# Down projection by seven half-size products in three of its four rounds

## The chip, the core and the metric

The kernel runs on one core of a Trainium2 chip, as one launch. The metric is the device time of that launch in microseconds (us). Five engines of the core matter here: TensorE (PE, matrix products; its weight loads are listed as PEld), VectorE (DVE), ScalarE (ACT), GpSimd (POOL) and the DMA queues, which are fed by SyncE (SP) and by GpSimd. Each engine takes its instructions in the order in which the program issues them, and waits on semaphores where an operand is not ready.

## What is computed

The reference is one decoder layer on 512 tokens of width 1024, in float32. The change touches its two feed-forward blocks only:

```python
D_MODEL = 1024; SEQ = 512; D_FF = 2816
def swiglu(x, w_gate, w_up, w_down):
    return (jax.nn.silu(x @ w_gate) * (x @ w_up)) @ w_down
h = h + 0.5 * swiglu(rms_norm(h, g_ffn1[i]), w_ffn1_gate[i], w_ffn1_up[i], w_ffn1_down[i])
...                                    # gated convolution and three-group attention, then
h = h + 0.5 * swiglu(rms_norm(h, g_ffn2[i]), w_ffn2_gate[i], w_ffn2_up[i], w_ffn2_down[i])
h = h + sigmoid(rmsnorm(h) @ W_pg) * (p[i] @ W_pp)
y = rmsnorm_final(h)
```

## The kernel before, in words

**Numbers.** Every matrix product is done three times at a reduced float32 (type fp32r): a weight w is split in wh (rounded) and wl (the rest), data in the same way, and wh·xh, wh·xl and wl·xh are added up in PSUM (`mm3`, L386). A weight is split by ACT (rounding) and DVE (the rest), or, for the products in `BY_DMA` and the slabs in `RAISED`, by ACT twice and an adding DMA that GpSimd issues: ACT writes -wh into wl, and the DMA adds w to it (`remainder`, L313). Such a slab is ready only when that DMA has landed.

**Layout.** Data lie transposed: a tile of 128 partitions holds 128 features, its 512 columns are the tokens. D_FF has 22 chunks of 128 features, which the code takes as 11 pairs j. Stationary operands are 128x128 blocks of weights; 1024 columns of them are a slab (`W`, 16 buffers, L232). All tiles of data come from one pool of 61 (`T`, L150).

**Gate and up.** The first two pairs (`EARLY`) are computed plainly with 512-column matmuls while the norm is still under way (`plain`, L573). For the other nine, gate and up together are a 2x2 block product: weights in quarters A11 to A22 (the two halves of the 1024 inputs for gate and for up), tokens in two halves. The block product is done by seven half-size products instead of eight (`PRODUCTS`, L66). The data's sums and differences of blocks are formed once (`normed`, L596); those of the weights are formed for each pair by four DVE operations (`sum_one`, L266). Each product is 4 x 2 x 3 = 24 matmuls of 256 columns, into one of three PSUM banks (pa, pe, pd), several products on top of each other; after each product the bank is read by ACT (copy) or DVE (sum), before the next product that adds to it (`gate_up`, L666). The hidden chunks of a pair are then split into hidh and hidl (`keep`, L566).

**Down.** Hidden chunks are multiplied by the down weights in three rounds of 8, 8 and 6 chunks. For each of the 8 output tiles m a round makes 8 x 3 (or 6 x 3) matmuls of 512 columns into a bank pd, and DVE adds half of it to the residual (`down`, L714). In the last round the residual is also split for the next stage and squared for its norm (`into`, L757).

**Order.** `PLAN` (L70) writes out the order of gate/up pairs and down rounds. Slabs are loaded, summed and split a fixed number of slabs ahead of their use (`slab`, L371): splitting by DMA begins 4 slabs ahead (`EARLIER`), the other splits 2 ahead. Small work is queued as `jobs`, and `work` (L554) takes them as far as an account of ACT and DVE time allows. The rotary tables of the attention (32 DVE operations, `tables`, L779) are put between the products of the first block from pair 3 on.

Of the kernel before, what the change touches and what calls it, by code (L numbers as in the profile page):

```python
# [52 lines left out]

N_TAB = {3: 1, 4: 1, 5: 1, 6: 1}
EARLIER = 4
MORE = 1
# [43 lines left out]

def ffn_order(n):
    out = [("gq", n, j, q) for j in range(EARLY) for q in range(4)]
    for step in PLAN:
        if step[0] == "gu":
            out += [(n, step, q) for q in PRODUCTS]
        else:
            out += [("d" + n, m, step[1]) for m in range(*step[2:])]
    return out
# [24 lines left out]
def block_kernel(ctx: ExitStack, tc: tile.TileContext, a, out):  # L133
    nc = tc.nc
    V, A, PE, G = nc.vector, nc.scalar, nc.tensor, nc.gpsimd

# [45 lines left out]
    def quarter(n, j, q):  # L182

        x_, y = divmod(q, 2)
        w = a["w_ffn%s_%s" % (n, ("gate", "up")[x_])]
        return [w[2 * j + i][:, y * S:(y + 1) * S] for i in range(2)]

    def source(key):
        kind = key[0]
        if kind in ("d1", "d2"):  # L190
            ks = ROUNDS[key[2]]
            return a["w_ffn%s_down" % kind[1]][key[1]][:, ks[0] * P:(ks[-1] + 1) * P]
# [8 lines left out]
    def sources(key):  # L201
# [7 lines left out]
        if key[0] == "gq":  # L209
            return row_of(quarter(*key[1:]))  # L210
# [42 lines left out]
    def load_one(hold=False):  # L253
# [5 lines left out]
        elif q == "B11":  # L259
            for z in (A21, A22, A11):  # L260
                quarters[key[:2], z] = fetch(row_of(quarter(key[0], key[1][1], z)))
        elif q == "B21":
            quarters[key[:2], A12] = fetch(row_of(quarter(key[0], key[1][1], A12)))
        state["load"] = i + 1

    def sum_one():  # L266
# [13 lines left out]
        if q in PRODUCTS[:4]:  # L280
            spend(0, 0.17 + w * 0.001)
        if q == "B11":
            r = z(A11)
            mixed[k, 1] = W("s1")[:, :w]
            V.tensor_add(mixed[k, 1], z(A21), z(A22))
        elif q == "B21":
            r = z(A12)
            mixed[k, 2] = W("s2")[:, :w]
            V.tensor_sub(mixed[k, 2], mixed[k, 1], z(A11))
        elif q == "T2":  # L290
            r = mixed[k, 2]
            s3 = z(A21, True)
            V.tensor_sub(s3, z(A11, True), s3)
            mixed[k, 3] = s3
        elif q == "T1":
            r = mixed.pop((k, 1))
            mixed[k, 4] = W("s4")[:, :w]
            V.tensor_sub(mixed[k, 4], z(A12, True), mixed.pop((k, 2)))
        elif q == "T3":
            r = mixed.pop((k, 3))  # L300
        elif q == "B22":
            r = mixed.pop((k, 4))
        else:
            r = z(A22, True)
# [65 lines left out]

    def slab(key):  # L371
# [4 lines left out]
        for j in range(i + 1, i + AHEAD + sums + 1):  # L376
            ahead("load", load_one, j + 1)
            ahead("sum", sum_one, j + 1)
            ahead("early", early_one, min(j, i + EARLIER) + 1)
            ahead("split", split_one, min(j, i + AHEAD) + 1)  # L380
        ahead("load", load_one, i + AHEAD + RAW + 1)
# [51 lines left out]
    def begin(norm):  # L433
# [8 lines left out]
        def piece(j, queue):  # L442
            for i, c in cuts[j]:
                g, at = divmod(c.start, S)
                src = quarter("1", 0, (A11, A12)[i])[g]
# [97 lines left out]
    jobs = []  # L543

    def job(f, a_=0.0, v=0.0):

        jobs.append((f, a_, v))

    def next_job():
        f, a_, v = jobs.pop(0)  # L550
        spend(a_, v)
        f()
# [7 lines left out]
    def ffn(n, xs, norm, resid, after):  # L560
        lo, hi = slice(0, 256), slice(256, 512)
        hid = []
        spare = []
        xn = [None] * 4

        def keep(ts):  # L566
            hl = [(T("hidh", F32R), T("hidl", F32R)) for _ in ts]
            for t, (h, l) in zip(ts, hl):
                job(lambda t=t, h=h: A.activation(h, t, AF.Copy), 0.63)
            for t, (h, l) in zip(ts, hl):  # L570
                job(lambda t=t, h=h, l=l: (V.tensor_sub(l, t, h.bitcast(F32)), hid.append((h, l))), v=0.69)
# [13 lines left out]
        def gated(pgs, pus, R):  # L585
# [8 lines left out]
            keep(tu)  # L594

        def normed(R):  # L596
# [26 lines left out]
            for c in range(4):  # L623
                xn[c] = {}
# [23 lines left out]
        for j in range(EARLY):  # L648
# [9 lines left out]
            gated(*done, R)  # L658
# [6 lines left out]

        def gate_up(j):  # L666
# [4 lines left out]
            us_ = W("u")  # L671
            both = us_.rearrange("p (c s) -> p c s", s=S)

            for q in PRODUCTS:
# [4 lines left out]
                for k in range(4):  # L679
                    th, tl = xn[k][q]  # L680
                    for g in range(2):
                        c = slice((g * 4 + k) * P, (g * 4 + k + 1) * P)
                        mm3(p[:, g * 256:(g + 1) * 256], h[:, c], l[:, c], th, tl,
                            q in ("B11", "B21", "T1") and k == g == 0, k == 3, True)
                m = N_TAB.get(j, 0) if n == "1" else 0
                background(m)
                spend(0, 0.7 * m)
                if j > EARLY:
# [5 lines left out]
                elif q == "T4":  # L694
                    while "gate" not in t:
# [4 lines left out]
                    keep([both[:, i] for i in range(2)])  # L700
                else:
# [5 lines left out]
                    elif q == "B22":  # L707
                        job(lambda z=z: A.activation(z, z, AF.Silu), 0.63)
                        job(lambda: V.tensor_mul(both[:, :, hi], t["T1"].rearrange("p (c s) -> p c s", s=256),
                                                 t["T2"].rearrange("p (c s) -> p c s", s=256)), 0, 0.69)  # L710
                if j == EARLY:
                    work(2.88)

        def down(r, first_, end):  # L714
            ks = ROUNDS[r]
            if n == "1" and r == len(ROUNDS) - 1:
                spare.append(T("h"))
            for m in range(first_, end):
                while len(hid) <= ks[-1] and m > first_:
                    next_job()  # L720
                p = bank("pd")
                key = "d" + n, m, r
                h, l = slab(key)
                for i, k in enumerate(ks):
# [747 lines left out]
```

## Time and profile before

| | |
|---|---|
| median of 3 runs | 1300.3 us (1300.05 to 1300.98) |
| the profiled execution's own time | 1300.78 us |
| its span (first to last instruction) | 1298.7 us |
| PE busy | 1285.4 us, 99% of the span |
| weight loads (PEld) | 1141.1 us, 88% |
| DVE busy | 835.1 us, 64% |
| ACT busy | 689.4 us, 53% |
| POOL busy (all of it DMA issues) | 231.9 us, 18% |
| mean granted TensorE clock | 0.998 |

The row of an instruction gives its start and its duration. [...] A group's row gives the busy time of the group, the mean of one instruction in ns, and the idle time in front of it with what ended it.

### The profile page before, as it was taken

The numbers are of one execution on the slowest core, as the hardware profiler recorded it, in microseconds if no ns is written. First come the engines' busy times: TensorE is split into PE (matmuls) and PEld (weight loads), VectorE is DVE, ScalarE is ACT, GpSimd is POOL, SyncE is SP. The second block draws the span as 40 slices with busy tenths as digits, with TensorE's granted clock in tenths as the row PEclk, the third lists the DMA queues.
The fourth block names the chain that finished last, engine by engine and source line by source line (L and its number), as shares of the span: only waits on it lengthen the run. The fifth ranks groups of instructions, "written<-read, shape, count | busy, mean of one in ns | idle before, by whom it ended". The sixth has DMA issues, their size and how long they took to land.

```text
span 1298.7 us, 19406 instructions
## 1 busy us (share of the span) xinstructions
PE 1285.4 (99%) x7474; PEld 1141.1 (88%) x7474; DVE 835.1 (64%) x1379; ACT 689.4 (53%) x989; POOL 231.9 (18%) x302
## 2 busy tenths in 40 slices
PE   9999999999999999999999999999999999999996
PEld 7899899898888888989898888888998899898886
DVE  6985567362559887878778757555972366352565
ACT  6667276565533264746556345343765367474552
POOL 3111111112232232323322210001102111111000
PEclk9999999999999999999999999999999999999999
DMA  9668766969888889898897782325669676868641
GB/s 300 144 158 228 195 154 160 227 149 223 203 200 199 201 149 197 166 186 152 173 182 169 175 226 86 97 92 137 146 149 251 169 181 156 216 161 199 158 103 60
DMA packets 106404, 223.35 MB, mean 172 GB/s; under 512 B 19272, under 2 KB 41160, under 8 KB 106312
## 3 DMA queue, kind: packets, MB, share of 16 engines
q0 software_dynamic: 47008, 135.29, 51.5%
q1 hardware_dynamic: 59016, 86.56, 21.2%
q8 instruction: 59, 0.97, 0.3%
q14 instruction: 33, 0.27, 0.1%
q10 hardware_dynamic: 288, 0.26, 0.1%
HBM read 164.36 MB, written 2.13 MB: 128 GB/s over the span
## 4 chain that ended last, share of the span: by engine, by line
PE 93%; DMA 3%; issue 2%; DVE 1%; ACT 0%; POOL 0%; SPq 0%; ACTq 0%; POOLq 0%; DVEq 0%
PE pd L387 8%; PE pd L388 8%; PE pd L389 8%; PE pa L389 6%; PE pa L387 6%; PE pa L388 6%; PE pq L387 4%; PE pq L388 4%; PE pq L389 4%; PE pg L387 3%; PE pg L388 3%; PE pg L389 3%; DMA wl<-wr 2%; PE pb L387 2%; PE pb L388 2%
## 5 line engine op out<-in xcount | busy, mean ns | idle before, releaser
L318 POOL DMA_DIRECT2D wl<-wr x106 | 91.3, 864 | 522.6 <-ACT wl L316 473.4
L862 DVE SCALAR_TENSOR_TENSOR acc<-glu,taps,acc 128x511 f32<-128x511 f32 (+14 forms) x240 | 161.5, 731 | 0.0
L316 ACT ACTIVATE wl<-wr 128x1024 fp32r<-128x1024 f32 (+1 forms) x106 | 108.1, 1020 | 80.1 <-DMA wl<-wr 40.6
L387 PE MATMUL pd<-hidh,wh 128*128 128x512 f32 x352 | 137.0, 389 | 0.0
L388 PE MATMUL pd<-hidl,wh 128*128 128x512 f32 x352 | 137.0, 389 | 0.0
L389 PE MATMUL pd<-hidh,wl 128*128 128x512 f32 x352 | 136.9, 389 | 0.0
L389 PE MATMUL pa<-bh,wl 128*128 128x256 f32 x432 | 122.7, 284 | 0.3 <-DVE wl L347 0.3
L387 PE MATMUL pa<-bh,wh 128*128 128x256 f32 x432 | 122.3, 283 | 0.4 <-ACT p L692 0.4
L388 PE MATMUL pa<-bl,wh 128*128 128x256 f32 x432 | 122.2, 283 | 0.0
L330 ACT ACTIVATE wh<-wr 128x1024 fp32r<-128x1024 f32 (+1 forms) x106 | 107.6, 1015 | 27.0 <-DMA wl<-wr 24.1
L347 DVE TENSOR_TENSOR wl<-s,wh 128x1024 fp32r<-128x1024 f32 x54 | 66.0, 1221 | 64.9 <-ACT wh L346 64.8
L316 ACT ACTIVATE wl<-wh 128x1024 fp32r<-128x1024 f32 x76 | 79.7, 1051 | 50.2 <-DMA wh<-in_w_in 38.9
L387 PE MATMUL pq<-xsh,wh 128*128 128x512 f32 x224 | 88.7, 396 | 0.0
L318 POOL DMA_DIRECT2D wl<-in_w_in x56 | 48.2, 860 | 222.1 <-ACT wl L316 221.0
L388 PE MATMUL pq<-xsl,wh 128*128 128x512 f32 x224 | 87.3, 390 | 0.0
L389 PE MATMUL pq<-xsh,wl 128*128 128x512 f32 x224 | 87.3, 390 | 0.0
L389 PEld LDWEIGHTS pa<-bh,wl 128*128 128x128 f32 x432 | 82.9, 192 | 0.9 <-DVE wl L347 0.6
L387 PEld LDWEIGHTS pa<-bh,wh 128*128 128x128 f32 x432 | 82.9, 192 | 0.6 <-ACT p L692 0.6
L388 PEld LDWEIGHTS pa<-bl,wh 128*128 128x128 f32 x432 | 82.9, 192 | 0.0
L387 PE MATMUL pd<-bh,wh 128*128 128x256 f32 x288 | 81.8, 284 | 0.4 <-ACT p L692 0.3
L389 PE MATMUL pd<-bh,wl 128*128 128x256 f32 x288 | 81.5, 283 | 0.0
L388 PE MATMUL pd<-bl,wh 128*128 128x256 f32 x288 | 81.5, 283 | 0.0
(302 smaller groups left out, 3572.0 us busy)
## 6 DMA issues: line engine op xcount, KB each, us to landing
wl<-wr POOLq DMA_DIRECT2D x90, 512.0 KB, 5.9
wh<-in_w_in POOLq DMA_DIRECT2D x56, 512.0 KB, 7.1
wl<-in_w_in POOLq DMA_DIRECT2D x56, 512.0 KB, 6.0
wr<-in_w_ffn_up SPq DMA_DIRECT2D x80, 256.0 KB, 4.1
wr<-in_w_ffn_gate SPq DMA_DIRECT2D x78, 256.0 KB, 4.5
wr<-in_w_ffn_down SPq DMA_DIRECT2D x32, 512.0 KB, 6.2
wr<-in_w_ffn_down SPq DMA_DIRECT2D x16, 384.0 KB, 7.6
wl<-wr POOLq DMA_DIRECT2D x16, 384.0 KB, 5.6
```

Of the source, the lines that this page charges most:

```text
L316: A.activation(l.bitcast(F32R), h, AF.Copy, scale=-1.0)
L318: G.dma_start(to, src, accum_op=OP.add)
L330: A.activation(h, r, AF.Copy)
L347: V.tensor_sub(l, r, h.bitcast(F32))
L387: PE.matmul(ps, wh, xh, start=start, stop=False, skip_group_check=part)
L388: PE.matmul(ps, wh, xl, start=False, stop=False, skip_group_check=part)
L389: PE.matmul(ps, wl, xh, start=False, stop=stop, skip_group_check=part)
L862: bg.append(lambda acc=acc, g=g, w=w, s=s: V.scalar_tensor_tensor(acc[:, s:], g[:, :S - s], w, acc[:, s:], op0=OP.mult, op1=OP.add))
```

## The change

In three of now four rounds, the down projection is computed as the gate/up is: the two halves of the round's chunks and two groups of output tiles are the blocks of the weights, the two halves of the tokens those of the data. The rounds are now (pairs) 0-1, 2-4, 5-7 and 8-10; the first, of four chunks, stays plain (`down_plain`) and is placed between the gate/up of pair 10 and the last round. A seven-product round is done in two halves g (output tiles 0, 1, 4, 5 and 2, 3, 6, 7), each of seven products of 3 x 2 x 3 = 18 matmuls of 256 columns on slabs of 768 columns.

For this, each pair of hidden chunks is turned into its blocks, sums and differences (`form`): four differences of 256 columns by GpSimd, and the splits of 256 + 3 x 512 columns by ACT and DVE, in place of two splits of 512 columns. The weights' sums and splits of a down unit are made as those of a gate/up pair. Each product's result is added to two residual tiles, half of their columns at a time (`add`).

Other edits: within a product all matmuls with wh come first, then all with wl (`quarters_of`), in gate/up too; the splits by DMA begin 3 slabs ahead for B11 and B21, 5 for T4 and 3 for plain slabs (`LEAD`, `NEXT`); queued jobs are taken after a bank has been read instead of before (`FIRST`); the forming of pairs is a second queue, `later`, from which fixed numbers are taken after each product (`QUOTA`, `AFTER`); the splits of pairs 0 and 1 move from the beginning to pairs 9 and 10; the table operations move to the last two seven-product rounds, pairs 9 and 10 and the plain round; in the last stage the norm's sum over features is taken two blocks later.

```diff
+LEAD = {"T4": 5, "B11": 3, "B21": 3}
+NEXT = 3
+FORMS_ = True
+FIRST = True
-ROUNDS = (range(8), range(8, 16), range(16, 22))
-PLAN = (("gu", 2), ("gu", 3), ("gu", 4), ("dn", 0, 0, 8), ("gu", 5), ("gu", 6), ("gu", 7), ("gu", 8),
-        ("dn", 1, 0, 4), ("gu", 9), ("gu", 10), ("dn", 1, 4, 8), ("dn", 2, 0, 8))
+ROUNDS = ((0, 2), (2, 3), (5, 3), (8, 3))
+PLAN = (("gu", 2), ("gu", 3), ("gu", 4), ("gu", 5), ("dn", 1, 0), ("dn", 1, 1), ("gu", 6), ("gu", 7), ("gu", 8),
+        ("dn", 2, 0), ("dn", 2, 1), ("gu", 9), ("gu", 10), ("dp", 0), ("dn", 3, 0), ("dn", 3, 1))
+AFTER = {"B11": 1, "B21": 1, "T2": 1, "T1": 1, "T3": 2, "B22": 2}
+TABLES = {"B21": 1, "T3": 1, "B22": 1, "T1": 1}
+TABLES_P = 1
+TABLES_D = {"B21": 1, "T3": 1, "B22": 1, "T4": 1}
+QUOTA = {"T4": 2, "B11": 3, "B21": 2, "T2": 1, "T1": 3, "T3": 3, "B22": 3}
-RAISED = ("d1", "d2", "v0")
+RAISED = ("dp", "v0")
...
+    FORMS = G if FORMS_ else V
...
+        at, k = ROUNDS[step[1]]
+        at = (2 * at + y * k) * P
+        return [a["w_ffn%s_down" % n][4 * x_ + 2 * step[2] + i][:, at:at + k * P] for i in range(2)]
...
+    def soon_(i, to):
+        while state["early"] < min(to + 1, len(order)):
+            j = state["early"]
+            lead = EARLIER if order[i][0] not in ("1", "2") else NEXT
+            if j - i > (LEAD.get(product(order[j]), 9) if product(order[j]) else lead):
+                break
+            early_one()
...
+        def form():
+            j, (x1, x2), tile_ = waiting.pop(0)
+            second, t = [], {"tile": tile_}
+            pairs[j] = {}
+            def sub(o, half, p_, q_):
+                def f():
+                    if o not in t:
+                        t[o] = T("t")
+                    FORMS.tensor_sub(t[o][:, half], p_(), q_())
+                job(f, v=0.43 if FORMS is V else 0, queue=later)
+            def put(names, src):
+                w, at = 256 * len(names), []
+                def first_():
...
+                    A.activation(at[0], src(), AF.Copy)
+                def end():
+                    V.tensor_sub(at[1], src(), at[0].bitcast(F32))
...
+            put(("B11",), lambda: x1[:, lo])
+            put(("B21", "B22"), lambda: x2)
+            sub(0, lo, lambda: x1[:, hi], lambda: x1[:, lo])
+            sub(0, hi, lambda: x2[:, hi], lambda: t[0][:, lo])
+            second.pop(0)()
+            put(("T1", "T2"), lambda: t[0])
+            second.pop(0)()
+            sub(1, lo, lambda: x2[:, hi], lambda: x1[:, hi])
+            sub(1, hi, lambda: x2[:, lo], lambda: t[0][:, hi])
+            second.pop(0)()
+            put(("T3", "T4"), lambda: t[1])
+            second.pop(0)()
...
+        def quarters_of(p, q, h, l, xs_):
+            w = len(xs_)
+            at = [(p[:, g * 256:(g + 1) * 256], slice((g * w + k) * P, (g * w + k + 1) * P), *x_)
+                  for k, x_ in enumerate(xs_) for g in range(2)]
+            for i, (o, c, th, tl) in enumerate(at):
+                PE.matmul(o, h[:, c], th, start=q in ("B11", "B21", "T1") and i == 0, stop=False, skip_group_check=True)
+                PE.matmul(o, h[:, c], tl, start=False, stop=False, skip_group_check=True)
+            for i, (o, c, th, tl) in enumerate(at):
+                PE.matmul(o, l[:, c], th, start=False, stop=i >= len(at) - 2, skip_group_check=True)
...
+        def add(m, half, p, into_=None):
+            p = p.rearrange("p (c s) -> p c s", s=256)
+            a_, b_ = resid[m], resid[m + 1]
+            if into_:
+                for i, t in enumerate((a_, b_)):
+                    V.scalar_tensor_tensor(classes(into_[i])[:, :, half.start // NB:half.stop // NB], by_class(p[:, i]), 0.5,
+                                           by_class(t[:, half]), op0=OP.mult, op1=OP.add)
+            elif b_.tensor is a_.tensor and b_.offset == a_.offset + S:
+                t = bass.AP(tensor=a_.tensor, offset=a_.offset, ap=[a_.ap[0], [S, 2], [1, S]])[:, :, half]
+                V.scalar_tensor_tensor(t, p, 0.5, t, op0=OP.mult, op1=OP.add)
+            else:
+                for i, t in enumerate((a_, b_)):
+                    V.scalar_tensor_tensor(t[:, half], p[:, i], 0.5, t[:, half], op0=OP.mult, op1=OP.add)
...
+        def down(r, g_):
+            at, k_ = ROUNDS[r]
+            ps = {q: bank(q) for q in ("pa", "pe", "pd")}
+            into_ = {"B11": "pa", "B21": "pe", "T2": "pa", "T1": "pd", "T3": "pa", "B22": "pd", "T4": "pa"}
+            goes = {"B11": (0, lo), "B21": (0, lo), "T2": (0, hi), "T1": (4, hi), "T3": (4, hi), "B22": (0, hi), "T4": (4, lo)}
+            last = r == len(ROUNDS) - 1
+            for q in PRODUCTS:
+                h, l = slab((n, ("dn", r, g_), q))
+                p = ps[into_[q]]
+                for k in range(k_):
+                    while q not in pairs.get(at + k, ()):
+                        next_job(later)
+                quarters_of(p, q, h, l, [pairs[at + k].pop(q) if g_ else pairs[at + k][q] for k in range(k_)])
+                m = goes[q][0] + 2 * g_
...
+                    add(m, goes[q][1], p)
+                if last and q in ("B22", "T4"):
+                    for i in range(2):
+                        job(lambda m=m + i: after[0](m), queue=later)
+                        squares.append((lambda m=m + i: after[1](m), 0, 0))
+                    if g_ and n == "1":
+                        flush(later)
...
+                elif last and g_:
+                    for _ in range(min(AFTER.get(q, 0), len(later))):
+                        next_job(later)
+                background(TABLES_D.get(q, 0))
+        def down_plain(r):
+            at, k_ = (2 * z for z in ROUNDS[r])
+            for m in range(KD):
...
+                    mm3(p, h[:, c], l[:, c], hid[at + i][0], hid[at + i][1], i == 0, i == k_ - 1)
+                V.scalar_tensor_tensor(resid[m], p, 0.5, resid[m], op0=OP.mult, op1=OP.add)
...
-            if j and b == 1:
+            if j and b == 3:
                 r = gnorm.by_token(diag=False)
```

More of the change, by code (lines that the diff above doesn't have):

```diff
@@ L98, with chunks @@
 ROUND = 12582912.0
+def chunks(j):
+    for at, k in ROUNDS:
+        if at <= j < at + k:
+            return at + j, at + j + k
 def ffn_order(n):
@@ L103, in ffn_order @@
     for step in PLAN:
-        if step[0] == "gu":
+        if step[0] == "dp":
+            out += [("dp", n, step[1], m) for m in range(0, KD, 2)]
+        else:
             out += [(n, step, q) for q in PRODUCTS]
-        else:
-            out += [("d" + n, m, step[1]) for m in range(*step[2:])]
     return out
@@ L303, in sum_one @@
         else:
[L304 removed]
+            quarters.pop((k, A22))
+            return
         raws[i] = r
@@ L573, in plain, with form_up_to @@
+        def form_up_to(j):
+            while waiting and waiting[0][0] <= j:
+                form()
         def plain(us_, beside):
@@ L678, in gate_up @@
                     next_job()
[L679 to L688, printed above, removed]
+                quarters_of(p, q, h, l, [z[q] for z in xn])
+                if j > EARLY and not FIRST:
                     work(2.88)
@@ new lines, in ffn, with flush @@
+        squares = []
+        def flush(queue, to=None):
+            while queue:
+                if to is None:
+                    next_job(queue)
+                else:
+                    to.append(queue.pop(0))
+        def down(r, g_):
[12 more added lines that the diff above has]
+                m = goes[q][0] + 2 * g_
+                if last and n == "1" and q in ("B21", "T3", "B22", "T4"):
+                    if not spare:
+                        spare.extend(T("h") for _ in range(4))
+                    new = spare[:2] if q in ("B21", "B22") else spare[2:4]
+                    add(m, goes[q][1], p, new)
+                    if q in ("B22", "T4"):
+                        spare.extend(resid[m:m + 2])
+                        resid[m:m + 2] = new
+                    if q == "T4":
+                        del spare[:4]
+                else:
+                    add(m, goes[q][1], p)
[5 more added lines that the diff above has]
+                        flush(later)
+                if last and g_ == 0 and q == "T4":
+                    flush(squares, later)
+                if last and g_ and q == "T4":
+                    flush(squares, later)
+                    if n == "1":
+                        flush(later)
+                elif last and g_:
+                    for _ in range(min(AFTER.get(q, 0), len(later))):
+                        next_job(later)
+                background(TABLES_D.get(q, 0))
+                work(k_ * 0.72)
@@ L1331, in block_kernel @@
             A.activation(pp[b, j], p, AF.Copy)
+            for _ in range(min(len(later), 3)):
+                next_job(later)
     pTh = pTl = wh = wl = None
```

162 lines of the change are left out of this document (91 added, 71 removed).

## The prediction, made before the changed kernel ran

> **What bounds the kernel now.** I read the head of the page and the summary of its chain first, then TensorE's list of waits.
>
> ```profile
> span 1298.7 us, 19406 instructions
> PE 1285.4 (99%) x7474; PEld 1141.1 (88%) x7474; DVE 835.1 (64%) x1379; ACT 689.4 (53%) x989; POOL 231.9 (18%) x302
> PEclk9999999999999999999999999999999999999999
> PE 93%; DMA 3%; issue 2%; DVE 1%; ACT 0%; POOL 0%; SPq 0%; ACTq 0%; POOLq 0%; DVEq 0%
> ...
> PE pa L387 <- ACT p L692: 0.4, 1, 0.4
> PE pd L387 <- ACT p L692: 0.3, 1, 0.3
> PE pa L389 <- DVE wl L347: 0.3, 1, 0.3
> ```
>
> TensorE is busy for 99% of the span, at full clock, and the waits of its half-size products (banks pa and pd), which make up most of the two feed-forward blocks, come to 1.0 us in all. So the time is that of the matmul stream: fewer or cheaper matmuls shorten it, and anything else counts only if it opens a gap in that stream. A busy share doesn't give the price of a matmul, since the durations overlap. I take it from the distances between starts in TensorE's timeline: two neighbouring products of gate/up, then the first matmul of the first down round and the first one behind it.
>
> ```profile
> 74.45 0.28 PE L387 MATMUL pa<-b,wh 128*128 128x256 f32 x1
> 74.57 0.28 PE L388 MATMUL pa<-b,wh 128*128 128x256 f32 x1
> 74.69 0.28 PE L389 MATMUL pa<-b,wl 128*128 128x256 f32 x1
> 74.81 0.28 PE L387 MATMUL pa<-b,wh 128*128 128x256 f32 x1
> ...
> 77.33 0.28 PE L387 MATMUL pe<-bh,wh 128*128 128x256 f32 x1
> ...
> 114.96 0.40 PE L387 MATMUL pd<-hidh,wh 128*128 128x512 f32 x1
> ...
> 158.51 0.28 PE L387 MATMUL pa<-b,wh 128*128 128x256 f32 x1
> ...
> L389 PE MATMUL pd<-hidh,wl 128*128 128x512 f32 x352 | 136.9, 389 | 0.0
> ```
>
> 24 matmuls of 256 columns take 77.33 - 74.45 = 2.88 us, 120 ns each. The round of 8 x 8 x 3 = 192 matmuls of 512 columns takes 43.55 us, 226.8 ns each. Half the columns thus cost 53% of the time, and that is the catch: seven half-size products for eight save 12.5% of the columns but 1 - 7/8 x 120/113.4 = 7.4% of the time. The group row gives the count: 352 matmuls for each of the three passes in two blocks, 528 a block.
>
> **The change, part by part.**
>
> *The matmul stream.* Before, a block's down projection is 528 x 226.8 ns = 119.8 us. After, the plain round of 4 chunks keeps 4 x 8 x 3 = 96 matmuls, 21.8 us, and three rounds are 2 x 7 x 18 = 252 matmuls of 256 columns each, 756 x 120 ns = 90.7 us. The difference is 7.3 us a block, **14.5 us** in two. The new order inside a product (all wh, then all wl) changes half the bank more often. In the rows above the third step, which changes weight and half, is as long as the others, 0.12 us; I take nothing for it.
>
> [...]
>
> *The blocks of the hidden pairs and the weights' sums.* These are the added operations, and they are hidden only as far as DVE, ACT and GpSimd have room beside TensorE. I read the room from one gate/up pair (the window row: length, then busy time of PE, PEld, DVE, ACT, POOL), and the prices from the groups.
>
> ```profile
> 178.67:198.83 20.16, 20.16 (x170) 20.16 (x169) 13.47 (x15) 13.45 (x17) 2.54 (x3) 1.00 0.73 183
> ...
> L347 DVE TENSOR_TENSOR wl<-s,wh 128x1024 fp32r<-128x1024 f32 x26 | 31.7, 1221 | 30.4 <-ACT wh L346 30.3
> L571 DVE TENSOR_TENSOR hidl<-u,hidh 128x512 fp32r<-128x512 f32 x18 | 11.9, 686 | 5.9 <-ACT hidh L569 5.9
> L738 DVE SCALAR_TENSOR_TENSOR gx<-pd,gx 128x512 f32<-128x512 f32 x16 | 10.9, 688 | 22.1 <-PE pd L389 22.1
> L620 DVE TENSOR_TENSOR t<-xn,t 128x256 f32<-128x256 f32 x8 | 3.4, 422 | 0.1
> ...
> L569 ACT ACTIVATE hidh<-u 128x512 fp32r<-128x512 f32 x18 | 10.6, 623 | 14.6 <-DVE u L709 13.3 <-DVE u L697 1.3
> ...
> L318 POOL DMA_DIRECT2D wl<-wr x106 | 91.3, 864 | 522.6 <-ACT wl L316 473.4 <-PE pd L388 25.5 <-DVE p L703 11.4
> ```
>
> In a gate/up pair (20.16 us) DVE loses two splits of 0.69 and gains 0.42 + 3 x 0.69: 13.5 becomes 14.6 us. ACT loses 2 x 0.62 and gains about 0.43 + 3 x 0.62: 13.4 becomes 14.5. Both keep 5.5 us of room; without that cover, DVE's 2.5 us for each of 18 pairs would be 45 us. A down unit lasts 126 x 0.12 = 15.1 us. In it DVE has four sums and four splits of 768 columns, 0.95 each (between 0.69 at 512 and 1.22 at 1024), and seven additions of 0.69, or 2 x 0.42 where the two residual tiles aren't neighbours: 12.4 to 13.5 us. That fits too, more tightly. A bank must be read before the product after the next one adds to it, within 2.16 us of its own end; in the program nothing but one sum and one split stand before the reading on DVE. I take zero for rounds 1 and 2.
>
> GpSimd's four differences of 128x256 have no row. The nearest rows are DVE's own, 0.42 us, and GpSimd's shortest steady work, a DMA issue of 0.86 us. Its queue has 17 us of room in the 20 (2.5 busy). Queued behind two of them stands the issue of the next pair's T4 split, now begun five slabs ahead, 14.4 us before its use, so 1.7 us of delay is harmless; B11's issue comes behind the other two. On the path: zero, with a loss as the bound (rival 3).
>
> *The end of the first block.* Here the cover is thin. The last down unit carries, beside its products, the splits and the norm's squares of the next stage, and a table operation after four products.
>
> ```profile
> L735 DVE SCALAR_TENSOR_TENSOR gx<-pd,gx 128x512 f32<-128x512 f32 x7 | 7.4, 1058 | 7.4 <-PE pd L389 7.4
> L408 DVE SCALAR_TENSOR_TENSOR xsl<-gx,xsh 128x512 fp32r<-128x512 f32 x7 | 5.3, 751 | 5.6 <-ACT xsh L407 5.6
> L504 DVE TENSOR_TENSOR sq<-sq,sq 128x512 f32<-128x512 f32 x7 | 4.8, 686 | 0.1
> L788 DVE TENSOR_SCALAR n<-n 128x512 f32<-128x512 f32 x3 | 1.3, 421 | 0.0
> L788 DVE SCALAR_TENSOR_TENSOR ang<-n,ang 128x512 f32<-128x512 f32 x6 | 4.1, 688 | 0.1
> ...
> 356.01 0.39 PE L387 MATMUL pb<-xsh,wh 128*128 128x512 f32 x1
> ...
> 363.49 0.95 PE L515 MATMUL ss<-mean,sq 128*128 128x1 f32 x8
> ```
>
> DVE's bill inside that unit: 4 x 0.95 for weights, 3 x 0.69 and 4 x 1.06 for additions (the reordering ones), 6 x 0.75 for splits, 4 x 0.69 for squares, 4 x 0.55 for tables: 19.6 us against 15.1. DVE ends up to 4.5 us late, and still has two splits and four squares to do, 4.2 us. The next stage asks for tile 6 after 18 matmuls, 4.1 us, and for the norm's sum 363.49 - 356.01 = 7.5 us after its start. Late by 4.5 + 4.2 - 7.5 = 1.2 us at the sum, and by 4.5 + 0.75 - 4.1 = 1.2 or a little more at tile 6: I take **+1.5 us**, bounds 0 (DVE's rows overlap a little back to back) and 4.5 (the lag holds TensorE by its banks). The second block has no tables, no reordering, and a stage behind it that needs no residual at first: zero.
>
> *Weights that are split by DMA.* Three ahead instead of four, of products that in a down unit last 2.16 instead of 2.88 us.
>
> ```profile
> 190.27 1.06 ACT L316 ACTIVATE wl<-wr 128x1024 fp32r<-128x1024 f32 x1 [0.18 <-PE pd L388]
> ...
> 198.83 0.28 PE L387 MATMUL pa<-b,wh 128*128 128x256 f32 x1
> ...
> wl<-wr POOLq DMA_DIRECT2D x90, 512.0 KB, 5.9
> wl<-wr POOLq DMA_DIRECT2D x16, 384.0 KB, 5.6
> ...
> L316 ACT ACTIVATE wl<-wr 128x768 fp32r<-128x768 f32 x8 | 6.7, 835 | 5.5 <-DMA wr<-in_w_ffn_down 5.5
> ...
> 230.62 8.41 DMA wl<-wr
> ...
> 256.42 7.82 DMA wl<-wr
> 264.29 0.39 PE pe L389
> ```
>
> The first two rows are B11 of one pair: ACT starts on it 8.6 us before TensorE does. One slab less leaves 5.7 us, but wl is now first used after 16 matmuls, 1.92 us in, instead of two: 7.6 us against 1.05 (ACT) + 0.3 + 5.9 (landing) = 7.3. In a down unit three products are 6.5 us, plus 12 x 0.12 = 1.4: 7.9 against 0.84 + 0.3 + 5.6 = 6.7. Both just hold at the median landing. The last rows show that landings of about 8 us occur around down rounds, one of them just in time at 264.29. There are 16 such places (six down units a block, and pairs 6 and 9). I take **+2 us**, bounds 0 and 16 x 1.8 = 29 us (8.4 instead of 5.6 at each, less the 1.0 to 1.2 in hand).
>
> *Moved steps.* The splits of pairs 0 and 1 (four operations each on ACT and DVE) leave the crowded beginning, where TensorE's waits quoted above lie, and go to pairs 9 and 10 with 5.5 us of room: **-1 us**, bounds -1 and 0. The tables' one load on SP and 32 operations go to later rounds, which the last unit of block one has paid for above.
>
> *Sum,* against the profiled execution's own 1300.8: -14.5 - 1 + 1.5 + 2 = -12, so 1288.8; the median of the runs lies 0.5 lower: **1288.3 us**.
>
> **The rivals.**
>
> 1. *Everything is hidden.* -14.5 - 1: **1284.8**. For it: the rooms of 5.5 us and the later use of wl. Against it: the unit with 19.6 us of DVE work in 15.1.
>
> 2. *The short leads are missed.* Late splits by 0.9 us at 16 places eat the gain: 1288.3 - 2 + 14.4, **1300.7**; at half of them, **1293.5**. For it: landings of 8 us. Against it: the down units issue three splits of 384 KB in 15.1 us, where before eight slabs of 512 KB followed each other through the same queue.
>
> 3. *GpSimd's differences hold DVE up.* Should DVE stand still while GpSimd reads its operands, each pair loses four times a difference's length, s, from DVE's 5.5 us of room. That is harmless up to s = 1.4 us; beyond it, 16 pairs pay 4 x (s - 1.4), the gain of 12 is gone at s = 1.6, and at s = 2 it is 16 x 2.4 = 38 us, **1326**, slower than before. Against it: the nearest rows are 0.42 and 0.86. [...] No row here shows it, since GpSimd does no arithmetic before. [...]
>
> 4. *DVE is late at the end of block one by more than I count,* with all its lag on the path and the norm behind it: 8.7 us instead of 1.5, **1295.5**.
>
> **How the numbers follow.** My own case (1286.5 to 1291) 0.45; rival 1, 0.22; rival 2, 0.18, a third of it without a measurable gain; rival 3, 0.07; rival 4, 0.08. A measurement of this kernel tells about 0.2%, 2.6 us, from no change: below 1297.7 is faster, above 1302.9 slower. Faster: 0.45 + 0.22 + 0.12 + 0.08 = 0.87, of which I keep 0.86; same 0.06; slower 0.08. The range runs from 1283 (rival 1, and a little for what a wait costs beyond its listed idle time) to 1297 (rival 4 and most of rival 2).
>
> **What would show it.** Right: 756 matmuls of 256 columns a block on the down weights at 120 ns, down stages of 15.1 us a unit and 21.8 us for the plain round; gate/up pairs still at 20.16 us; TensorE's waits in the first pairs gone; GpSimd's differences below 1 us; a wait for DVE's squares or splits near the end of block one. Wrong: waits on wl's DMA at the first products of units (rival 2), DVE rows that lengthen while GpSimd works (rival 3), pairs longer than 20.2 us, or waits for a free slab or data tile, for which no row of before gives a price.

## The result, and the profile after

The changed kernel takes **1288.67 us** (median of 4 runs, 1287.96 to 1289.66) against 1300.41 us (1300.05 to 1300.98): a ratio of **0.991**, 95% interval 0.9893 to 0.9927, 11.7 us less. The prediction said 1288.3. The profiled execution took 1287.96 us. One execution of those below, in the run with the differences three times over, took 2542.6 us, against 1337.7 to 1340.6 of the four others, and is left out.

The head of the page of the changed kernel, then TensorE's list of waits (line waited at, what for: total us, times, longest):

```profile
span 1286.2 us, 21394 instructions
PE 1271.6 (99%) x8122; PEld 1158.6 (90%) x8122; DVE 1003.5 (78%) x1592; ACT 726.9 (57%) x1065; POOL 283.8 (22%) x370
...
PE ss L551 <- DVE sq L540: 1.1, 1, 1.1
PE pd L425 <- DMA wl<-wr: 1.0, 2, 0.6
PE pp L1498 <- DVE wl L389: 0.6, 1, 0.6
...
PE pa L763 <- DVE gx L828: 0.4, 1, 0.4
```

TensorE still bounds the kernel, with more matmuls (8122 for 7474) that are shorter. The waits of the first pairs for ACT are gone; four waits of 0.4 us or more are new in the two blocks or right behind them: the norm's squares behind block one (ss), the weights of the plain round (pd), the first weights behind block two (pp), one bank reading in the last unit of block one (pa).

Where the 12.5 us of span went is read from four stretches of each kernel: block one from its first half-size product, what follows it, block two likewise, and the rest (window: length, then busy time of PE, PEld, DVE, ACT, POOL; clock, DMA share, GB/s). The kernel before:

```profile
52.83:356.01 303.18, 302.38 (x2042) 280.80 (x2040) 175.19 (x222) 178.80 (x225) 47.18 (x57) 1.00 0.78 188
356.01:925.45 569.44, 569.44 (x2870) 484.76 (x2868) 419.34 (x766) 269.81 (x434) 130.00 (x174) 1.00 0.73 163
925.45:1227.82 302.37, 302.02 (x2042) 280.78 (x2040) 156.84 (x188) 176.78 (x220) 41.14 (x49) 1.00 0.76 185
1227.82:1298.70 70.88, 60.78 (x305) 52.50 (x304) 42.08 (x118) 31.18 (x60) 0.00 (x0) 0.97 0.29 75
```

The changed kernel, and behind its stretches one gate/up pair and one down unit:

```profile
52.43:348.34 295.91, 294.79 (x2365) 290.25 (x2364) 252.29 (x309) 194.17 (x257) 71.72 (x90) 1.00 0.77 183
348.34:919.64 571.30, 570.23 (x2870) 484.53 (x2869) 425.55 (x780) 273.42 (x441) 130.96 (x175) 1.00 0.74 164
919.64:1214.38 294.74, 294.31 (x2366) 290.06 (x2364) 236.90 (x293) 194.71 (x256) 67.60 (x83) 1.00 0.76 182
1214.38:1286.20 71.82, 61.74 (x306) 52.39 (x304) 47.05 (x125) 32.37 (x63) 0.00 (x0) 0.95 0.28 74
163.39:183.55 20.16, 20.16 (x171) 20.16 (x170) 15.48 (x16) 13.33 (x18) 4.71 (x6) 1.00 0.74 183
133.15:148.27 15.12, 15.12 (x129) 15.12 (x128) 11.88 (x16) 8.01 (x10) 2.54 (x3) 1.00 0.81 189
```

The blocks give 7.27 and 7.63 us; the start gives 0.40; the stretch behind block one takes 1.86 us more and the one behind block two 0.94: -0.40 - 7.27 - 7.63 + 1.86 + 0.94 = -12.5. Inside the blocks next to nothing is lost: 2268 matmuls at 0.12 us and 96 at 0.2268 are 293.9 us, so 2.0 us of block one and 0.8 of block two are stalls (before: 9 x 168 x 0.12 + 528 x 0.2268 = 301.2, so 2.0 and 1.2). A pair and a unit last exactly their matmuls, 168 x 0.12 and 126 x 0.12. DVE's load in block one rose from 175 to 252 us without making them longer.

A second profile of the changed kernel (the repeat among the experiments) has a start of 52.65 us and 295.78, 571.27, 294.81 and 72.66 us for the four stretches. The two blocks and what lies between them repeat within 0.2 us. The last stretch doesn't, by 0.84 us; what both profiles have there is the wait of 0.57 us at pp.

### The profile page after: what moved, and what is told of

It is laid out like the page before. It is cut to its first block, busy times and chain, and to the rows that moved or that the text cites. A ratio compares the mean times of both kernels' runs of the same rounds, so it can differ in the third digit from the quotient of the medians.

```text
span 1286.2 us, 21394 instructions
## 1 busy us (share of the span) xinstructions
PE 1271.6 (99%) x8122; PEld 1158.6 (90%) x8122; DVE 1003.5 (78%) x1592; ACT 726.9 (57%) x1065; POOL 283.8 (22%) x370
## 3 DMA queue, kind: packets, MB, share of 16 engines
q8 instruction: 64, 1.05, 0.3%
## 4 chain that ended last, share of the span: by engine, by line
PE 73%; DVE 3%; DMA 1%; issue 1%; ACT 1%; POOL 0%; ACTq 0%; POOLq 0%; DVEq 0%
PE pa L763 4%; PE pa L766 4%; PE pa L764 4%; PE pq L423 4%; PE pq L424 4%; PE pq L425 4%; PE pg L423 3%; PE pg L424 3%; PE pg L425 3%; PE pd L766 2%; PE pd L764 2%; PE pd L763 2%; PE pb L425 2%; PE pb L423 2%; PE pb L424 2%; PE pg L1514 1%
## 5 line engine op out<-in xcount | busy, mean ns | idle before, releaser
L763 PE MATMUL pa<-bh,wh 128*128 128x256 f32 x648 | 159.6, 283 | 0.5 <-DVE gx L828 0.4
L764 PE MATMUL pa<-bl,wh 128*128 128x256 f32 x648 | 159.4, 283 | 0.0
L372 DVE TENSOR_TENSOR wl<-s,wh 128x1024 fp32r<-128x1024 f32 (+1 forms) x90 | 101.0, 1124 | 38.0 <-ACT wh L371 37.7
L763 PEld LDWEIGHTS pa<-bh,wh 128*128 128x128 f32 x648 | 124.4, 192 | 0.9 <-issue 0.5
L764 PEld LDWEIGHTS pa<-bl,wh 128*128 128x128 f32 x648 | 124.4, 192 | 0.0
L341 ACT ACTIVATE wl<-wr 128x1024 fp32r<-128x1024 f32 (+1 forms) x102 | 99.5, 976 | 26.6 <-DVE wl L372 12.5
L371 ACT ACTIVATE wh<-s 128x1024 fp32r<-128x1024 f32 (+1 forms) x90 | 86.8, 964 | 34.0 <-PE pd L424 13.4
L766 PE MATMUL pa<-bh,wl 128*128 128x256 f32 x648 | 92.4, 283 | 0.0
L763 PEld LDWEIGHTS pd<-bh,wh 128*128 128x128 f32 x432 | 82.9, 192 | 0.0
L764 PEld LDWEIGHTS pd<-bl,wh 128*128 128x128 f32 x432 | 82.9, 192 | 0.0
L423 PE MATMUL pg<-xsh,wh 128*128 128x512 f32 x192 | 76.0, 396 | 0.4 <-ACT xsh L443 0.4
```

The lines of the kernel that those rows point to most:

```text
L341: A.activation(l.bitcast(F32R), h, AF.Copy, scale=-1.0)
L371: A.activation(h, r, AF.Copy)
L372: V.tensor_sub(l, r, h.bitcast(F32))
L423: PE.matmul(ps, wh, xh, start=start, stop=False, skip_group_check=part)
L763: PE.matmul(o, h[:, c], th, start=q in ("B11", "B21", "T1") and i == 0, stop=False, skip_group_check=True)
L764: PE.matmul(o, h[:, c], tl, start=False, stop=False, skip_group_check=True)
```

## The experiments

The ratio is always to the kernel before on the same chip.

### The order inside a product, undone

```diff
-                PE.matmul(o, h[:, c], th, start=q in ("B11", "B21", "T1") and i == 0, stop=False, skip_group_check=True)
-                PE.matmul(o, h[:, c], tl, start=False, stop=False, skip_group_check=True)
-            for i, (o, c, th, tl) in enumerate(at):
-                PE.matmul(o, l[:, c], th, start=False, stop=i >= len(at) - 2, skip_group_check=True)
+                mm3(o, h[:, c], l[:, c], th, tl, q in ("B11", "B21", "T1") and i == 0, i >= len(at) - 2, True)
```

> The changed kernel, with the three matmuls of each block in the old order (wh, wh, wl, block by block) instead of all wh first; nothing else differs. So wl is needed 1.7 us earlier in a gate/up product and 1.2 us earlier in a down product. The prediction's own sum (leads of 5.7 and 6.5 us against 6.7 to 7.3 us for the split and its landing) says that only the later use covers the shorter leads: 16 first products late by about 1.0 to 1.5 us, ratio to the kernel before 0.999 to 1.005. Rival, from the changed kernel's trace, where wl landed 1.94 us or more before its use at all 60 first and second products: still at least 0.2 us early, ratio 0.990 to 0.993. A third reading, that the new order itself makes matmuls cheaper or dearer: spacing of the 256-column matmuls other than 120 ns.

Measured: 1296.3 us, ratio 0.9964 (0.9952 to 0.9977), some 7 us slower than the changed kernel (7.6 by the medians, 7.0 by the ratios). TensorE's longest waits in this run, and a row of its chain of waits (start, duration):

```profile
PE pd L424 <- DVE hidl L611: 3.2, 2, 2.0
...
PE pe L425 <- DMA wl<-wr: 1.5, 3, 0.7
PE pa L425 <- DMA wl<-wr: 1.0, 1, 1.0
PE pd L425 <- DMA wl<-wr: 0.9, 2, 0.6
PE pa L425 <- DVE wl L372: 0.7, 1, 0.7
...
1126.01 5.66 DMA wl<-wr
```

The landing that begins at 1126.01 ends at 1131.67, and the product B21 of pair 9 takes its first wl there. Both expectations missed: the prediction's own sum for the old order was too dark, the reading from the trace too bright. Late wl is waited for at five gate/up products (of pairs 6, 8 and 10 in block one, 6 and 9 in block two; banks pe and pa above, 3.2 us), and at no down unit. The waits on pd's wl are those of the plain round, which the changed kernel has too. As much again, 3.2 us, is waited in the plain round for DVE's split of its chunks (hidl): before it DVE stands idle for 3.35 and 2.93 us, until the plain round's first wl has landed. Why the old order brings that stand about was not followed up. What follows: the short leads are harmless because of the later use of wl, and the new order is worth about 7 us here, some half of it at the products whose weights are late.

### The order alone, in the kernel before

```diff
+            for i, (o, c, th, tl) in enumerate(at):
+                PE.matmul(o, h[:, c], th, start=q in ("B11", "B21", "T1") and i == 0, stop=False, skip_group_check=True)
+                PE.matmul(o, h[:, c], tl, start=False, stop=False, skip_group_check=True)
+            for i, (o, c, th, tl) in enumerate(at):
+                PE.matmul(o, l[:, c], th, start=False, stop=i >= len(at) - 2, skip_group_check=True)
...
-                        mm3(p[:, g * 256:(g + 1) * 256], h[:, c], l[:, c], th, tl,
-                            q in ("B11", "B21", "T1") and k == g == 0, k == 3, True)
+                quarters_of(p, q, h, l, [z[q] for z in xn])
```

(the kernel before, in its gate/up products)

> The kernel before, with only the new order of matmuls (all wh, then all wl) in its gate/up products; the down projection stays plain. Theory: the gain of the change is the down projection's; this order does no more than take away the two waits of about 0.5 us for wl that the trace of before shows in its first and later pairs: 0 to -1 us, ratio 0.999 to 1.000, spacing 120 ns. Rival (a good part of the measured 12 us comes from the other edits): -3 us or more, ratio 0.9975 or less.

Measured: 1299.36 us, ratio 0.9988 (0.998 to 0.9997): 1.5 us gained, with the long leads of before. So the order by itself is not where the 12 us come from; together with the run above, it is what allows short leads.

### The pairs' differences back on DVE

```diff
-FORMS_ = True
+FORMS_ = False
```

> The changed kernel, with the four differences of each pair made by DVE instead of GpSimd. Theory (GpSimd's differences hold up DVE's operations with two operands in SBUF): DVE gains 72 x 0.42 = 30 us of work and loses the stretched rows, about 1.5 us a pair or 27 us, so DVE's busy time stays near 1003 us, and the two stretched groups of splits go back from 1.54 and 1.06 us to 0.69 and 0.42; time unchanged, ratio 0.990 to 0.992. Rival (the long rows come from something else, such as waiting for ACT): they stay long, and DVE's busy time rises by 30 us to 1033; if DVE's room were already used up by that, the time would rise by several us, ratio 0.995 or more.

Measured: 1288.07 us, ratio 0.9905 (0.989 to 0.992), no difference from the changed kernel. But DVE got *less* busy by doing 72 operations more. The groups of the pairs' splits on DVE and of the differences (count, busy us, mean ns), in the changed kernel:

```profile
L641 DVE TENSOR_TENSOR bl<-u,bh 128x512 fp32r<-128x512 f32 x18 | 28.4, 1580 | 0.0
L641 DVE TENSOR_TENSOR b<-u,b 128x256 fp32r<-128x256 f32 x18 | 17.8, 990 | 0.0
...
94.05 0.73 POOL L626 TENSOR_TENSOR t<-u 128x256 f32<-128x256 f32 x1 [4.56 <-DVE u L793]
...
99.31 1.02 POOL L626 TENSOR_TENSOR t<-u 128x256 f32<-128x256 f32 x1
100.01 1.01 POOL L626 TENSOR_TENSOR t<-u,t 128x256 f32<-128x256 f32 x1
99.39 2.18 DVE L641 TENSOR_TENSOR bl<-u,bh 128x512 fp32r<-128x512 f32 x1
```

and in this run:

```profile
PE 1271.7 (99%) x8122; PEld 1158.2 (90%) x8122; DVE 992.7 (77%) x1664; ACT 727.4 (57%) x1065; POOL 228.3 (18%) x298
...
L626 DVE TENSOR_TENSOR t<-u,t 128x256 f32<-128x256 f32 x36 | 15.2, 421 | 0.4
L626 DVE TENSOR_TENSOR t<-u 128x256 f32<-128x256 f32 x36 | 15.1, 419 | 0.0
L641 DVE TENSOR_TENSOR bl<-u,bh 128x512 fp32r<-128x512 f32 x18 | 12.3, 684 | 0.0
L641 DVE TENSOR_TENSOR b<-u,b 128x256 fp32r<-128x256 f32 x18 | 7.5, 419 | 0.0
```

The DVE split that starts 0.08 us after a GpSimd difference lasts 2.18 us instead of 0.68. It ends 0.55 us after the second of GpSimd's two differences, as if it had stood still until GpSimd was through; without differences on GpSimd such splits take 0.68 us in the mean. The 30.3 us that GpSimd takes over are paid back in splits that last longer (26.4 us in these two groups) and in other operations; DVE's total falls by 10.8 us when it does the work itself. The expectation had it unchanged.

### The differences three times over

```diff
-                    FORMS.tensor_sub(t[o][:, half], p_(), q_())
+                    for _ in range(3):
+                        FORMS.tensor_sub(t[o][:, half], p_(), q_())
```

> The changed kernel, with each GpSimd difference done three times into the same tile (same result). GpSimd's own work per pair becomes 12 x 0.73 to 1.0 plus 2.5 us of DMA issues, 11 to 15 us of 20.2, so by its own queue there is room. Theory of the hold: eight more operations a pair can hold DVE by up to 0.73 to 1.0 each; DVE has 4 to 5 us left of 20.16, so 1 to 4 us a pair go over, 16 to 60 us in all, ratio 1.003 to 1.04, and slower than before. If only the operations that happen to meet are held, the excess stays inside the room: ratio 0.991 to 1.000 with DVE's busy time up by 30 us or more. Rival (no hold): DVE's busy time unchanged at about 1003, ratio 0.990 to 0.993.

Measured: 1339.1 us (median of four executions), ratio 1.0293 (1.0279 to 1.0307), some 50 us slower than the changed kernel. The groups on GpSimd, TensorE's waits, and one of ACT's:

```profile
L627 POOL TENSOR_TENSOR t<-u,t 128x256 f32<-128x256 f32 x108 | 138.2, 1280 | 6.7
L627 POOL TENSOR_TENSOR t<-u 128x256 f32<-128x256 f32 x108 | 109.1, 1010 | 49.3 <-DVE u L794 43.6
...
PE pa L764 <- DVE p L802: 22.0, 15, 2.6
PE pd L425 <- DMA wl<-wr: 7.9, 2, 4.3
...
ACT bh L639 <- POOL t L627: 97.4, 35, 6.3
```

So the way to a slower kernel existed: with some 3.4 us for each difference (three of 1.01 or 1.28) DVE reads the banks late and TensorE waits for it. But the hold is only part of it. DVE's busy time grows by 30.0 us (1033.5 against 1003.5). ACT stands 97.4 us for the differences themselves, which it has to round next (3.5 us in the changed kernel), and what stands behind them on its queue comes later. And PE is busy 16.8 us longer with the same matmuls (1288.4 against 1271.6), at a mean granted clock of 0.989. How much of the 50 us the hold alone costs, this run doesn't show. At one difference, DVE's room swallows the hold, as the run before this one shows.

### The changed kernel again, and with plain slabs split four ahead

> The changed kernel once more, as the measure for the runs beside it: ratio to the kernel before 0.990 to 0.992, about 1288.5 us.

Measured: 1290.71 us, ratio 0.9913 (0.9899 to 0.9927); the kernel before took 1301.68 us beside it. With the other lead:

```diff
-NEXT = 3
+NEXT = 4
```

> The changed kernel, with the plain slabs' split by DMA begun four slabs ahead again instead of three (NEXT 4); the seven-product slabs keep their leads. Theory: the short lead costs only where a plain slab stands behind a half-size product, at the first slab of the plain round, where TensorE waited 0.58 and 0.43 us (steps 0.75 and 0.60 us longer): 1.3 us less than the changed kernel, ratio lower by 0.001, and the two waits gone. Rival (the wait comes from a free slab, not from the lead): the waits stay or move to the next slab, no change.

Measured: 1290.72 us, ratio 0.9913 (0.99 to 0.9927): nothing. TensorE no longer waits for the plain round's first slab; two matmuls later it waits as long for DVE's split of the round's chunks (first row, both blocks). The second row is of DVE:

```profile
PE pd L424 <- DVE hidl L611: 1.0, 2, 0.5
...
302.48 0.96 DVE L309 TENSOR_TENSOR s<-wr,wr 128x768 f32<-128x768 f32 x1 [5.35 <-DMA wr<-in_w_ffn_down]
```

In the repeat of the changed kernel both limits show, one behind the other: the step for the weights is 0.28 us too long, the one for the split 0.25 us, in each block. The split is finished no earlier than the weights had landed before, so an earlier landing alone gains nothing. And in this run the weights of the last round arrive later: DVE stands 5.35 us before its first sum of them (4.86 in block two), which it does nowhere in block one of the changed kernel.

### The tables earlier, with slabs four ahead

```diff
-NEXT = 3
+NEXT = 4
-TABLES_P = 1
+TABLES_P = 2
```

> As the run before it, and the table operations two per tile in the plain round (TABLES_P 2), so that none is left for the last round of block one. Theory (DVE's bill of 19.6 us in the last down unit makes the norm's sum late): 2.2 us of DVE work leave that unit and 2.2 the one before; the wait of 1.06 us for the squares (a step 1.2 us longer) and the one of 0.37 us for a bank go, 1.5 us less again, 1285.5 to 1286.5, ratio about 0.9885. Rival (the wait is set by ACT or by the order of the squares behind the splits): the wait stays at 1 us, no change against the run before it.

Measured: 1297.56 us, ratio 0.9967 (0.9955 to 0.9978): 6.8 us *slower* than the run before. One wait of TensorE carries most of it:

```profile
PE pa L763 <- DVE gx L828: 5.9, 1, 5.9
...
303.31 0.96 DVE L309 TENSOR_TENSOR s<-wr,wr 128x768 f32<-128x768 f32 x1 [6.12 <-DMA wr<-in_w_ffn_down]
...
322.73 0.68 DVE L899 SCALAR_TENSOR_TENSOR gx<-pd,gx 128x512 f32<-128x512 f32 x1
...
326.37 0.96 DVE L372 TENSOR_TENSOR wl<-s,wh 128x768 fp32r<-128x768 f32 x1 [1.10 <-ACT wh L371]
327.24 0.68 DVE L828 SCALAR_TENSOR_TENSOR gx<-pa,gx 128x512 f32<-128x512 f32 x1
```

DVE has stood 6.1 us for late weights, and has six table operations more than the run before (14 for 8) up to the reading at 322.73; the plain round's last bank, whose matmuls ended at about 317.7, is read at 322.73. Behind it come the last table operations, which pass between DVE and ACT, and a split that waits 1.10 us for ACT; the reading that TensorE needs starts at 327.24. In the 15.75 us behind the plain round (317.65 to 333.40), the wait among them, the mean granted clock is 0.78, against 1.00 in that round (295.01 to 317.65); how much of the 6.8 us that is was not shown. The lead of four slabs alone had cost nothing; the table edit alone was not run, so that it takes both to cost this is likely and not shown. It also means that this run says nothing on the squares: the wait for them stayed at 1.1 us.

### Four table operations moved, slabs three ahead

```diff
-TABLES = {"B21": 1, "T3": 1, "B22": 1, "T1": 1}
+TABLES = {"B11": 1, "B21": 1, "T2": 1, "T1": 1, "T3": 1, "B22": 1}
...
-                background(TABLES_D.get(q, 0))
+                background(TABLES_D.get(q, 0) if not last or len(bg) > 1 or g_ and q == "T4" else 0)
```

> The changed kernel with four of its table operations moved from the last round of block one into pairs 9 and 10 (six products of a pair take one, not four), and the last of them, the one that makes ACT and DVE wait for each other, kept behind the last product. In the changed kernel DVE finishes the norm's squares at 357.5 us of the span and TensorE could have used them at about 356.4: a wait of 1.06 us, the only one listed at the end of block one beside 0.4 us for a bank reading at the start of the last round. Theory (DVE's bill inside the last unit is what makes the squares late): three operations of 0.4 to 0.7 us leave the last unit, the squares are done about 1.7 us earlier, the wait for them is gone and the span is 1.0 to 1.5 us shorter, about 1285: a ratio near 0.990, a difference from the changed kernel that shows in the trace and hardly in the times. Rival (the squares hang on the last bank reading and on ACT, which come when they come): the wait for the squares stays at about 1 us. Second rival (the pairs 9 and 10, where DVE is busy for 18.1 of 20.16 us, have no room for two more operations each): waits for DVE's bank readings appear there, of 0.5 us and more, and the span doesn't get shorter.

Measured: 1288.34 us, ratio 0.9899 (0.9884 to 0.9914), by the times no different from the changed kernel; block one takes 295.21 us, 0.70 less, without the wait for the bank reading:

```profile
52.49:347.70 295.21, 294.58 (x2365) 290.18 (x2364) 252.47 (x310) 193.90 (x257) 72.34 (x90) 1.00 0.76 183
```

But the wait for the squares stays. DVE at the end of block one, changed kernel first (its last unit ends, and the next stage begins, at 348.34):

```profile
346.38 1.17 DVE L824 SCALAR_TENSOR_TENSOR gx<-pd,gx 128x256 f32<-128x256 f32 x2 [0.28 <-PE pd L766]
...
353.61 3.87 DVE L540 TENSOR_TENSOR sq<-sq,sq 128x512 f32<-128x512 f32 x5
...
357.62 1.02 PE L551 MATMUL ss<-mean,sq 128*128 128x1 f32 x8 [1.06 <-DVE sq L540]
```

then this run (stage at 347.70):

```profile
345.75 1.16 DVE L824 SCALAR_TENSOR_TENSOR gx<-pd,gx 128x256 f32<-128x256 f32 x2 [1.00 <-PE pd L766]
...
356.64 1.02 PE L551 MATMUL ss<-mean,sq 128*128 128x1 f32 x8 [1.05 <-DVE sq L540]
```

In both, DVE has caught up at the reading of B22's bank: it waits for TensorE there, 0.28 and 1.00 us. What is late is the row of work behind that reading, about 11 us long, which starts when TensorE's product ends, whatever DVE did earlier. The rival was right on the squares. The second rival's waits in pairs 9 and 10 don't appear.

### With the first weights behind block two split earlier as well

```diff
-                    for _ in range(min(AFTER.get(q, 0), len(later))):
+                    for _ in range(min(AFTER.get(q, 0) if n == "1" or q != "B22" else 0, len(later))):
-FORMS_ = True
+FORMS_ = False
```

(on top of the run before)

> As the run before, and two edits more: the pairs' differences go back to DVE, and in block two no queued job is taken after the product B22 of the last unit, so that the split of the first weights of the next stage no longer stands behind two squares on DVE (in the changed kernel TensorE waits 0.57 us for it at 1215.7). Theory: that wait goes, a further 0.6 us; the differences on DVE cost nothing, as measured, and leave DVE more room in pairs 9 and 10, so that waits for bank readings that the run before may show there go: a span of about 1284.5, 1.5 to 2 us below the changed kernel's, ratio 0.989. Rival: what DVE does later there is only asked for later (the splits of the residual behind the first products, 1228), and the time after block two stays at 71.8 us: a span of 1285 to 1286.

Measured: 1289.3 us, ratio 0.9904 (0.9887 to 0.992); no gain. The profiled execution is the slowest of the four (1292.6; the others took 1288.9 to 1289.4). In it the wait for pp's weights is gone, but the two squares that were put off are now waited for (0.98 us at 1225.41), the weights of the last stage came later, and in 3.4 us behind block one the granted clock was 0.52:

```profile
PE pg L1512 <- ACT pgh L379: 3.3, 1, 3.3
...
357.60:361.00 3.40, 3.40 (x10) 2.59 (x9) 3.02 (x19) 2.79 (x3) 2.12 (x4) 0.52 0.30 35
```

The block stages themselves have fewer stalls than in any other run (a span of 294.8 and 294.7 us from first product to next stage), but 1 us is below what the times resolve. What made the last stage's weights late here was not followed up; the same wait is 1.5 us with slabs four ahead and 0.4 us in the run before, so it isn't this edit's alone. None of these versions beats the changed kernel measurably.

### One of the three rounds plain again

```diff
-NEXT = 3
+NEXT = 4
-        ("dn", 2, 0), ("dn", 2, 1), ("gu", 9), ("gu", 10), ("dp", 0), ("dn", 3, 0), ("dn", 3, 1))
+        ("dp", 2), ("gu", 9), ("gu", 10), ("dp", 0), ("dn", 3, 0), ("dn", 3, 1))
...
+            if j in range(5, 8):
+                hl = [(T("hidh", F32R), T("hidl", F32R)) for _ in range(2)]
...
```

(the lines left out load this round's slabs by one output tile and split its chunks without blocks and differences)

> As the run with four slabs ahead, with the second seven-product round (pairs 5 to 7, three splits each of two chunks instead of blocks and differences) done plainly again in both blocks: 144 matmuls of 512 columns at 226.8 ns, 32.7 us, instead of 252 of 256 columns at 120 ns, 30.2 us. Theory (the gain is the matmul stream): 2 x 2.4 = 4.8 us more than the run with four slabs ahead, ratio higher by 0.0037. Rival 1 (other edits make the gain): no more than 1 us of difference. Rival 2 (the seven products cost more in stalls than their stream shows, or gain more): less than 3 or more than 7 us.

Measured: 1296.86 us, ratio 0.9959 (0.9947 to 0.9972), 6.1 us above the run that differs from it by this round alone. Here are the plain round and the two block stages, and behind them the block stages of that other run:

```profile
224.02:256.69 32.67, 32.67 (x146) 27.04 (x145) 13.10 (x19) 11.44 (x14) 5.62 (x7) 1.00 0.89 212
52.59:350.89 298.30, 297.22 (x2257) 287.01 (x2256) 226.29 (x282) 186.96 (x245) 64.61 (x80) 1.00 0.77 183
922.21:1219.42 297.21, 296.76 (x2257) 286.94 (x2256) 208.39 (x258) 187.62 (x246) 59.84 (x73) 1.00 0.76 183
...
52.53:348.41 295.88, 294.80 (x2366) 290.23 (x2364) 252.13 (x309) 193.77 (x256) 72.24 (x91) 1.00 0.76 182
921.83:1216.63 294.80, 294.35 (x2365) 290.13 (x2364) 235.31 (x293) 194.17 (x256) 67.14 (x83) 1.00 0.76 182
```

The round takes 32.67 us where two units take 30.24. Against the run with slabs four ahead the blocks are 2.42 and 2.41 us longer, 4.8 us in all: a third of the 14.5, as the matmul counts say. The other 1.3 us of the 6.1 lie outside the blocks and within what two such medians differ by.

## Why the prediction was right

The time agrees to 0.4 us, but not every term does.

- **The matmul stream, -14.5: right.** Spacings are 120 and 226.8 ns, the changed order costs nothing in the stream, and one round is worth 2.42 us a block (measured alone) where a third of the predicted 7.3 is 2.42.
- **The pairs' blocks and the weights' sums, 0: right,** as the rows of 20.16 and 15.12 us show. DVE's 15.5 us in a pair is above the 14.6 worked out; one split in it lasts 2.77 us beside three differences (at 170.61), 0.42 us in the mean with no differences on GpSimd; the unit's 11.9 lies below the 12.4 to 13.5.
- **GpSimd's differences, 0: right, by a margin that was mis-stated.** s is 0.73 us alone and about 1.02 when the two engines meet. Two of the prediction's own signs went against it: the differences are not below 1 us, and DVE's rows lengthen while GpSimd works (a split of 2.18 us against 0.68). So rival 3's hold shows in the rows; what kept it harmless is DVE's room (15.48 us busy of 20.16 in a pair). Its formula (beyond s = 1.4, 16 pairs, of the 18 that there are, pay 4 x (s - 1.4)) would give about 130 us at 3.4 us; some 50 were measured, and not by the hold alone. DVE does not stand still for every difference: 21 of the 72 meet none of its operations, and 20 of these last 0.73 to 0.75 us; its sum with a bank at 270.99, one operand in PSUM, takes 0.68 us inside a difference (270.69 to 271.71), the mean of its group.
- **Weights that are split by DMA, +2: too much.** The term's bounds had landings of 8 us at 16 places; at the down units they took 4.5 us (median, 384 KB) against the 5.6 worked with, and no product of a unit waited:

```profile
wl<-wr POOLq DMA_DIRECT2D x36, 384.0 KB, 4.5
```

  The 1.0 us that is waited for lies at the first slab of the plain rounds, which the step didn't name, and splitting earlier there gained nothing. Rival 2 described the kernel with the old order better than this one, and that only in part: late wl costs 3.2 us of waits there and not 14.4, and at gate/up pairs, not at down units.
- **Moved steps, -1: right in size.** The waits for ACT in the first pairs are gone. With +2 and -1 the prediction had +1 us for these two terms; the start and the blocks, less the 14.5 of the stream, gave -0.40 - 14.90 + 14.54 = -0.76. The 1.8 us between are what the steps missed most, by too dark a view of the DMA.
- **The end of block one, +1.5: 1.86 measured, for another reason.** The step had DVE up to 4.5 us late from a bill of 19.6 us in 15.1. DVE is behind inside the unit, which costs 0.4 us at one bank, but has caught up at the last bank but one. The wait of 1.06 us is the tail behind B22's reading: T4's two additions, four splits, seven sums of squares. Taking the table operations out of the unit left it where it was. That the size was right was luck.
- **The end of block two, 0: wrong by 0.94** (1.8 in the second profile, with the same wait)**.** The step looked for readers of the residual and not for what stands behind the new jobs on DVE's queue: the first weights of the next stage are split after two squares, and TensorE waits 0.57 us for them at 1215.7. Ordering them the other way round moved the wait to the squares (0.98 us). What else is longer in that stretch stays open.

Too dark by 1.8 and too bright by 0.36 + 0.94 leave 0.5: the terms' errors cancel, and so the sum is better than its parts. That it agrees to 0.4 us is luck; that the stream's 14.5 us nearly all arrive is not.

## What to carry to other kernels

Half-size products save by the price of the small matmul, not by their columns: take both spacings from the trace first (here 120 and 226.8 ns: 7.4% of a round instead of 12.5%). An order that needs a late operand last bought lead time for nothing here (the spacing stayed 120 ns); it was worth about 7 us with leads of three slabs, and 1.5 us with four in the gate/up products of the kernel before. When a queue is nearly full, look at what it catches up with and where it next waits for TensorE: moving work away from ahead of that point gained next to nothing here, the row of work behind it was waited for in every version, and where DVE had stood for a late load, more work in front of a bank's reading became a wait of 5.9 us.

## What the runs showed of the hardware

In the changed kernel GpSimd's differences and VectorE's splits, which read two tiles in SBUF, lengthen each other: a split of 0.68 us lasts 2.18 us beside differences that grow from 0.73 to 1.02 us. Moving 30 us of VectorE's work to GpSimd made VectorE 11 us *busier*. And the granted clock of TensorE fell in several executions, in two of them in a stretch that holds or follows a wait of TensorE. Behind the wait of 0.92 us for the squares of block one it was 0.52 for 3.4 us in the combined run, where matmuls of 512 columns come 0.43 us apart instead of 0.23. It was 0.78 from 317.65 to 333.40, around the wait of 5.9 us, in the run with the tables earlier, and 0.989 over the whole of the run with the differences three times over (0.997 in the changed kernel). In the first profile of the changed kernel, 1.00 was granted right behind the wait of 1.06 us for the squares (357.60 to 361.50), and with four table operations moved the matmuls behind the wait of 1.05 us come 0.23 us apart: the length of the wait alone doesn't decide it.
